# The output projection of a Hymba-style block as seven block products instead of eight

## The chip, the cores and the metric

The kernel runs on one core of a Trainium2 chip. The metric is device time in microseconds (us) of one execution, less is better. PE is the tensor engine, DVE the vector engine, ACT the scalar engine, POOL GpSimd, SP the engine whose queue issues the DMAs.

## The reference, cut to what matters

```python
mod = c_act @ w_ada[l] + b_ada[l]
shift, scale, gate = jnp.split(mod, 3, axis=-1)
h = _rms(x, norm_g[l]) * (1.0 + scale[:, None, :]) + shift[:, None, :]
proj = h @ w_in[l]
...
att = att * jax.nn.silu(a_z)
hg = _hgrn2(g_q, g_f, g_i, lbs[l], hg_norm_g[l]) * jax.nn.silu(g_z)
y = jnp.concatenate([att, hg], axis=-1) @ w_out[l]
x = x + gate[:, None, :] * y
```

1024 tokens, width 2048, all in float32; `w_in` is 2048 x 8192, `w_out` 2048 x 2048. There are 8 attention heads (`att`) and 8 recurrent heads (`hg`), each 128 wide.

## The kernel before

Every large product is made of three matmuls. Each float32 factor is split into a high and a low part: ACT copies it to the rounded type (`whi`), DVE subtracts that from the original (`wlo`). PE then adds high·high, high·low and low·high in PSUM.

The **input projection** goes through slices of `w_in`, four per head pair: `all` twice (q, k, v, i of half the tokens each), `qf` and `zz`. A slice has 16 row blocks of 128 (k tiles), 12 matmuls of 512 columns each. Weight tiles come through a small ring: `W.dma(n + 4)` loads four tiles ahead and `W.split(n + 2)` splits two ahead, with 4 buffers for the raw tile and 3 each for `whi` and `wlo`. The **mixers** of each head (attention, recurrence) are generators, traced in steps between these matmuls. A small planner (`Stream`, `Engine`, `run_ready`) estimates when each engine gets through its instructions and lets a mixer take its next step when its inputs should be there. What is fixed in this way is only the order on each engine; each engine then runs its own list strictly in that order. A further generator, `gate_gen`, forms the residual's gate and stores it to DRAM (`gdr`); it is done early.

The gated outputs of 14 of the 16 heads are put by in DRAM (`odr`) and come back in the last slice, two per k step (`reload_o`), as high and low parts; the last pair stays in SBUF.

The **output projection** multiplies these, 1024 tokens x 2048, with `w_out` in five column blocks (`outs`): two of 256 columns, then three of 512. The 256-wide blocks keep four PSUM banks busy while the last heads' mixers still hold the others; the 512-wide ones take all eight. For each head the ring brings a tile of `w_out`, PE multiplies it with the 8 token tiles, and after 16 heads DVE multiplies with the gate, adds x and SP stores. For the last block the gate is multiplied into `w_out` beforehand. The gate's sums over the partitions (`gate_rows`, the PSUM tile `gb`) are made in the first block:

```python
    outs = [(0, 256), (256, 512)] + [(c0, c0 + 512) for c0 in range(512, D, 512)]
...
            if kk in (8, 10, 12) and c0 == 0:
                gr = gate_rows() if kk == 8 else gr
                next(gr)
```

`big` is a pool of 14 SBUF tiles of 4 KB per partition (`T4`), `hp` one of 32 that holds the split h, later the split outputs.

## Time and profile before

| what | value |
|---|---|
| median of 3 runs | 2079.76 us (2079.02 to 2082.41) |
| profiled execution: first to last instruction (span) | 2077.0 us |
| median above that span | 2.76 us |
| PE busy in the span | 2046.1 us (99%) |
| DVE, ACT, POOL busy | 48%, 30%, 5% |
| DMA | 210.76 MB, mean 101 GB/s |

The span is counted from the first to the last instruction of one profiled execution. Its own device time is not recorded apart from that; what lies around the span is seen only as the 2.76 us by which the median of the other runs is longer. A matmul's record is longer than the distance to the next one, since matmuls are pipelined: its pace is read from start to start.

### The profile page before, as it was taken

Reading aid. Unit: us, or ns where it says so; the run is one execution under the profiler, and the core shown is the slowest. Engines: PE = TensorE matmul, PEld = TensorE weight load, DVE = VectorE, ACT = ScalarE, POOL = GpSimd, SP = SyncE. Lnnn points to the kernel's source line nnn. Section 1 sums busy time; section 2 is a strip of 40 time slices with the busy share of each in tenths; the row PEclk is TensorE's granted clock in tenths of the full one; section 3 lists DMA queues with packets and bytes.
Section 4 is the critical chain, followed back from the end, with each engine's and each line's share of the span. In section 5 each row is a group of like instructions: output and inputs, shape, how many; then the busy total and the mean of one; then the engine's idle time right before and its main releaser. Section 6 shows DMA issues by size and latency. Waiting matters only on the chain.

```text
span 2077.0 us, 30591 instructions
## 1 busy us (share of the span) xinstructions
PE 2046.1 (99%) x11905; PEld 1707.8 (82%) x11905; DVE 989.6 (48%) x1726; ACT 628.8 (30%) x1491; POOL 97.6 (5%) x104
## 2 busy tenths in 40 slices
PE   6999999999999999999999999999999999999999
PEld 4678878888888888888888888888888889988887
DVE  6884654475547443644363436343634384213142
ACT  6454323322431233124312431243134342111110
POOL 2440000000000000000000000000000000000000
PEclk9999999999999999999999999999999999999999
DMA  9982134334433331133113311331133152332231
GB/s 344 338 231 77 44 102 131 90 92 132 130 88 96 111 89 51 42 92 87 48 47 92 89 46 42 98 88 41 42 107 85 47 177 72 107 102 86 92 127 56
DMA packets 282485, 210.76 MB, mean 101 GB/s; under 512 B 17042, under 2 KB 255714, under 8 KB 282340
## 3 DMA queue, kind: packets, MB, share of 16 engines
q1 hardware_dynamic: 282084, 208.75, 33.5%
q8 instruction: 93, 1.52, 0.3%
q14 instruction: 52, 0.43, 0.1%
q0 software_dynamic: 256, 0.06, 0.0%
HBM read 191.96 MB, written 16.79 MB: 101 GB/s over the span
## 4 chain that ended last, share of the span: by engine, by line
PE 96%; DVE 1%; DMA 1%; ACT 0%; issue 0%; POOL 0%; SPq 0%; ACTq 0%; POOLq 0%; DVEq 0%
PE pj L87 63%; PE pjo L87 11%; PE po L87 6%; PE att L87 6%; PE pjn L87 2%; PE pjC L87 2%; PE lv L87 2%; PE hgo L87 1%; PE pjB L87 1%; PE qkT L87 1%; PE hgU L87 1%; DMA x<-in_x_dram 1%; PE xTp L87 1%; DMA wada<-in_w_ada_dram 0%; PE hgoT L87 0%
## 5 line engine op out<-in xcount | busy, mean ns | idle before, releaser
L87 DVE TENSOR_TENSOR wlo<-wraw,whi 128x512 fp32r<-128x512 f32 x440 | 303.2, 690 | 664.0 <-ACT whi L87 662.8
L87 ACT ACTIVATE whi<-wraw 128x512 fp32r<-128x512 f32 x440 | 276.8, 630 | 826.3 <-PE pj L87 514.5
L87 PE MATMUL pj<-hh,whi 128*128 128x512 f32 x1024 | 412.3, 403 | 0.0
L87 PE MATMUL pj<-hl,whi 128*128 128x512 f32 x1024 | 400.3, 391 | 0.0
L87 PE MATMUL pj<-hh,wlo 128*128 128x512 f32 x1024 | 399.7, 390 | 0.0
L87 PE MATMUL pj<-whi,hh 128*128 128x512 f32 x896 | 356.3, 398 | 0.5 <-DVE z L87 0.5
L87 PE MATMUL pj<-whi,hl 128*128 128x512 f32 x896 | 349.7, 390 | 0.0
L87 PE MATMUL pj<-wlo,hh 128*128 128x512 f32 x896 | 349.2, 390 | 0.0
L87 PEld LDWEIGHTS pj<-hl,whi 128*128 128x128 f32 x1024 | 192.2, 188 | 41.8
L87 PEld LDWEIGHTS pj<-hh,whi 128*128 128x128 f32 x1024 | 192.5, 188 | 36.2
L87 PEld LDWEIGHTS pj<-hh,wlo 128*128 128x128 f32 x1024 | 192.8, 188 | 34.2
L87 PEld LDWEIGHTS pj<-whi,hl 128*128 128x128 f32 x896 | 168.2, 188 | 35.7
L87 PEld LDWEIGHTS pj<-whi,hh 128*128 128x128 f32 x896 | 168.5, 188 | 34.4 <-DVE z L87 1.8
L87 PEld LDWEIGHTS pj<-wlo,hh 128*128 128x128 f32 x896 | 168.6, 188 | 31.8
L87 PE MATMUL pjo<-whi,oh 128*128 128x256 f32 (+1 forms) x448 | 147.7, 330 | 0.0
L87 PE MATMUL pjo<-whi,ol 128*128 128x256 f32 (+1 forms) x448 | 147.2, 329 | 0.0
L87 PE MATMUL pjo<-wlo,oh 128*128 128x256 f32 (+1 forms) x448 | 147.2, 328 | 0.0
L87 ACT ACTIVATE P<-att,mstat 128x640 f32<-128x640 f32 (+2 forms) x64 | 42.3, 662 | 167.3 <-DVE mstat L87 167.3
L87 PEld LDWEIGHTS pjo<-wlo,oh 128*128 128x128 f32 x448 | 84.6, 189 | 7.6
L87 PEld LDWEIGHTS pjo<-whi,oh 128*128 128x128 f32 x448 | 84.6, 189 | 7.6
L87 PEld LDWEIGHTS pjo<-whi,ol 128*128 128x128 f32 x448 | 84.6, 189 | 7.5
L87 PE MATMUL po<-whi,oh 128*128 128x512 f32 x192 | 74.7, 389 | 0.0
(223 smaller groups left out, 2283.0 us busy)
## 6 DMA issues: line engine op xcount, KB each, us to landing
wraw<-in_w_in_dram SPq DMA_DIRECT2D x240, 192.0 KB, 2.9
wraw<-in_w_in_dram SPq DMA_DIRECT2D x272, 128.0 KB, 2.6
wada<-in_w_ada_dram SPq DMA_DIRECT2D x64, 512.0 KB, 7.5
wadag<-in_w_ada_dram SPq DMA_DIRECT2D x64, 256.0 KB, 2.9
wraw<-in_w_in_dram SPq DMA_DIRECT2D x240, 64.0 KB, 2.7
wraw<-in_w_out_dram SPq DMA_DIRECT2D x48, 256.0 KB, 2.8
x<-in_x_dram SPq DMA_DIRECT2D x16, 512.0 KB, 10.1
xr<-in_x_dram SPq DMA_DIRECT2D x16, 512.0 KB, 6.5
```

The source lines that it names most:

```text
L87: return f(*a, **kw)
```

## The change

Write A for the heads' outputs and B for `w_out` times the gate. The change cuts A by tokens (first and last 512) and by kind of head (`att`, `hg`), B by kind of head and by column halves of 512 within a group `q` of 1024 columns, so that for each `q` a 2 x 2 by 2 x 2 block product remains. It is formed from seven products instead of eight (Strassen's scheme):

```
M1 = (A11+A22)(B11+B22)   M2 = (A21+A22) B11   M3 = A11 (B12-B22)   M4 = A22 (B21-B11)
M5 = (A11+A12) B22        M6 = (A21-A11)(B11+B12)                  M7 = (A12-A22)(B21+B22)
C11 = M1+M4-M5+M7   C12 = M3+M5   C21 = M2+M4   C22 = M1-M2+M3+M6
```

The right factors are formed by a new generator, `wout_gen`, that runs after the gate has been stored, among the mixers of the middle heads: 16 rounds (2 `q` x 8 `j`), each with two loads of 512 KB of `w_out`, two multiplications with the gate (1024 wide), five additions (512 wide) and seven stores of 256 KB to the DRAM tile `wdr`. The left factors are formed in `out_sums`, five additions per head pair as it comes back (`reload_o`, now four loads of 256 KB). The output projection is then 2 x 7 products of 8 steps; a step loads one right tile (256 KB), splits it, splits one left tile (`ahl`) and does 12 matmuls of 512 columns into four banks, two sets of four in turn. The sums of the M's, x and the stores lie among the steps of M6 and M7 (`finals`), the copies out of PSUM at each product's last step. The last head pair takes its slices in the order `qf`, `all`, `all`, `zz`. Comments were removed as well.

```diff
+OUTPACE = 20.0
...
-                if len(self.specs[self.ns]) == 4:       # times the gate
-                    c0 = self.specs[self.ns][3]
-                    V.tensor_mul(raw, raw, gates[c0 // 1024][:, c0 % 1024:c0 % 1024 + 512].rearrange(
-                        "p (a b) -> p a b", a=2))
...
+    OA = {}
+    def half_tile(j):
+        if j % 2 == 0:
+            OA["half"] = hp.tile([128, 1024], F32, tag="h", name="oah")
+        return OA["half"][:, (j % 2) * 512:(j % 2) * 512 + 512]
+    def out_sums(j, a11, a12, a21, a22):
+        y, z = (hp.tile([128, 1024], F32, tag="h", name=n) for n in ("oay", "oaz"))
+        a7 = half_tile(j)
+        V.tensor_add(y[:, 512:1024], a21, a22)
+        V.tensor_add(y[:, 0:512], a11, a22)
+        V.tensor_add(z[:, 0:512], a11, a12)
+        V.tensor_sub(z[:, 512:1024], a21, a11)
+        V.tensor_sub(a7, a12, a22)
+        OA[j] = {1: y[:, 0:512], 2: y[:, 512:1024], 3: a11, 4: a22, 5: z[:, 0:512], 6: z[:, 512:1024], 7: a7}
     def finish(kt, oT, direct):
         if direct:
-            hi = hp.tile([128, 1024], F32R, tag="h", name=f"oh{kt}")
-            lo = hp.tile([128, 1024], F32R, tag="h", name=f"ol{kt}")
-            A.activation(hi, oT, AF.Copy)
-            V.tensor_sub(lo, oT, hi.bitcast(F32))
-            O[kt] = (hi, lo)
+            O[kt] = oT
+            if len(O) == 2:
+                a, b = O[NH - 1], O[2 * NH - 1]
+                out_sums(NH - 1, a[:, 0:512], b[:, 0:512], a[:, 512:1024], b[:, 512:1024])
         else:
             DMA.dma_start(odr[slot[kt]], oT)
...
+        wait(10.0)
+        yield
+        yield from wout_gen()
+    def wout_gen():
+        for q in range(2):
+            a, hi, lo = T4("gl"), T4("ghi", dt=F32R), T4("glo", dt=F32R)
+            DMA.dma_start(a, gdr[q])
+            A.activation(hi, a, AF.Copy)
+            V.tensor_sub(lo, a, hi.bitcast(F32))
+            yield
+            p = MA("gb")
+            for s in (slice(0, 512), slice(512, 1024)):
+                PE.matmul(p[:, s], onesr.to_broadcast([128, 128]), hi[:, s], start=True, stop=False)
+                PE.matmul(p[:, s], onesr.to_broadcast([128, 128]), lo[:, s], start=False, stop=True)
+            gate = T4("gateb")
+            A.activation(gate, p, AF.Copy)
+            gate = gate.rearrange("p (a b) -> p a b", a=2)
+            yield
+            for j in range(NH):
+                r1, r2 = T4("wor", (128, 2, 512)), T4("wor", (128, 2, 512))
+                for r, e in ((r1, 2 * j), (r2, 2 * j + 1)):
+                    DMA.dma_start(r.rearrange("p a b -> p (a b)"), wout_v[:, order[e], q * 1024:(q + 1) * 1024])
+                wait(OUTPACE)
+                yield
+                V.tensor_mul(r1, r1, gate)
+                yield
+                V.tensor_mul(r2, r2, gate)
+                yield
+                b11, b12, b21, b22 = r1[:, 0, :], r1[:, 1, :], r2[:, 0, :], r2[:, 1, :]
+                for ma, mb, fa, fb in ((1, 3, (V.tensor_add, b11, b22), (V.tensor_sub, b12, b22)),
+                                       (4, 6, (V.tensor_sub, b21, b11), (V.tensor_add, b11, b12))):
+                    o = T4("wos", (128, 2, 512))
+                    fa[0](o[:, 0, :], *fa[1:])
+                    yield
+                    fb[0](o[:, 1, :], *fb[1:])
+                    wait(2.0)
+                    yield
+                    DMA.dma_start(wdr[q, ma - 1, j], o[:, 0, :])
+                    DMA.dma_start(wdr[q, mb - 1, j], o[:, 1, :])
+                    if ma == 1:
+                        DMA.dma_start(wdr[q, 1, j], b11)
+                        DMA.dma_start(wdr[q, 4, j], b22)
+                V.tensor_add(b21, b21, b22)
+                wait(2.0)
+                yield
+                DMA.dma_start(wdr[q, 6, j], b21)
+    def wait(us):
+        Engine.cur.t = max(Engine.cur.t, PE.free) + us
...
-        slices += [("all", h, 0), ("all", h, 1)] if h else []
-        slices += [("qf", h, 0), ("zz", h, 0)]
+        al = [("all", h, 0), ("all", h, 1)] if h else []
+        slices += al + [("qf", h, 0), ("zz", h, 0)] if h < NH - 1 else [("qf", h, 0)] + al + [("zz", h, 0)]
...
-    for c0, c1 in outs:
-        first["o", c0] = len(specs)
-        st_ = 512 // (c1 - c0)
-        for kk in range(0, NK, st_):
-            specs.append((wout_v, tuple(order[kk:kk + st_]), list(range(c0, c1, 128))) + ((c0,) if c1 == D else ()))
...
+    wdr = dr.tile([2, 7, NH, 128, 512], F32, name="wdr")
...
             W.split(n + 2)
     def reload_o(j):
-        kt = order[j]
-        a = T4("orl")
-        DMA.dma_start(a, odr[slot[kt]])
-        hi = hp.tile([128, 1024], F32R, tag="h", name=f"oh{kt}")
-        lo = hp.tile([128, 1024], F32R, tag="h", name=f"ol{kt}")
-        A.activation(hi, a, AF.Copy)
-        V.tensor_sub(lo, a, hi.bitcast(F32))
-        O[kt] = (hi, lo)
+        oa, ob = (odr[slot[order[i]]] for i in (2 * j, 2 * j + 1))
+        x_ = hp.tile([128, 1024], F32, tag="h", name="oax")
+        r = T4("orl")
+        DMA.dma_start(x_[:, 0:512], oa[:, 0:512])
+        DMA.dma_start(x_[:, 512:1024], ob[:, 512:1024])
+        DMA.dma_start(r[:, 0:512], ob[:, 0:512])
+        DMA.dma_start(r[:, 512:1024], oa[:, 512:1024])
+        out_sums(j, x_[:, 0:512], r[:, 0:512], r[:, 512:1024], x_[:, 512:1024])
+    CHAIN = ((2, 0, True), (3, 1, True), (4, 0, False), (5, 1, False), (1, 0, True), (6, 1, True), (7, 0, False))
+    steps = [(q, m, j) for q in range(2) for m, _, _ in CHAIN for j in range(NH)]
+    raws, wsp, asp = {}, {}, {}
+    def right_dma(n):
+        for i in range(len(raws), min(n + 1, len(steps))):
+            q, m, j = steps[i]
+            raws[i] = wp.tile([128, 512], F32, tag="wraw", name="wraw", bufs=4)
+            DMA.dma_start(raws[i], wdr[q, m - 1, j])
+    def right_split(n):
+        right_dma(n)
+        for i in range(len(wsp), min(n + 1, len(steps))):
+            hi = wp.tile([128, 512], F32R, tag="whi", name="whi")
+            lo = wp.tile([128, 512], F32R, tag="wlo", name="wlo")
+            A.activation(hi, raws[i], AF.Copy)
+            V.tensor_sub(lo, raws[i], hi.bitcast(F32))
+            wsp[i] = (hi, lo)
+    def left_split(n):
+        for i in range(len(asp), min(n + 1, len(steps))):
+            _, m, j = steps[i]
+            while j not in OA:
+                PE.free += 0.5
+                run_ready()
+            hl = T4("ahl", (128, 2, 512), F32R)
+            A.activation(hl[:, 0, :], OA[j][m], AF.Copy)
+            V.tensor_sub(hl[:, 1, :], OA[j][m], hl[:, 0, :].bitcast(F32))
+            asp[i] = hl
...
-                    reload_o(2 * kk - 2)
-                    reload_o(2 * kk - 1)
+                    reload_o(kk - 1)
+                if sl == slices[-1] and kk >= 6:
+                    right_dma(2 * kk - 10)
+                    right_split(kk - 6)
+                    left_split(kk - 6)
...
-                    for t in (2 * b, 2 * b + 1):
-                        for i in range(2):
-                            ohi, olo = O[order[kk + i]]
-                            nat_unit(nat[b][:, t % 2, :], ohi, olo, t, w, i, kk + i, t % 2 == 0)
...
+    banks = [[pj.tile([128, 512], F32, tag="pj", name="pjo") for _ in range(4)], None]
+    n = 0
+    for q in range(2):
+        C = {}
+        for m, s_, fresh in CHAIN:
+            if s_ == 1 and banks[1] is None:
                 mx_ctx.__exit__(None, None, None)
                 po_ = ctx.enter_context(tc.tile_pool(name="po", bufs=4, space=PSUM))
+                banks[1] = [po_.tile([128, 512], F32, tag="po", name="po") for _ in range(4)]
+            for j in range(NH):
+                for u in range(4):
+                    if u == 0:
+                        right_dma(n + 4)
+                        right_split(n + 2)
+                    if u == 2:
+                        left_split(n + 2)
+                    right_split(n)
+                    left_split(n)
+                    (whi, wlo), hl = wsp[n], asp[n]
+                    b = banks[s_][u]
+                    ts = slice(u * 128, (u + 1) * 128)
+                    first, last = fresh and j == 0, j == NH - 1
+                    PE.matmul(b, hl[:, 0, ts], whi, start=first, stop=False, skip_group_check=True)
+                    PE.matmul(b, hl[:, 0, ts], wlo, start=False, stop=False, skip_group_check=True)
+                    PE.matmul(b, hl[:, 1, ts], whi, start=False, stop=last, skip_group_check=True)
                     run_ready()
+                    if last:
+                        if m == 2:
+                            if u == 0:
+                                C["v"] = res("cv")
+                            A.activation(C["v"][u], b, AF.Copy, scale=-1.0)
...
+                    elif m in (6, 7) and u in (1, 3):
+                        next(later, None)```

**Start of the output projection, PE.** Rows of the change's instruction order, matmul result<-moving,stationary. Before, the last slice (`pj`) is followed by a step of the last recurrent head's mixer (`lv`) and by 256-wide matmuls, two heads to a tile of weights:

```order
L87 MATMUL pj_13944<-hl15_1616,whi_14205 128x512
L87 MATMUL lv_14321<-hgQ_13914,hgK_13915 32x32 x16
L87 MATMUL pjo_14422<-whi_14253,oh0_14024 128x256
L87 MATMUL pjo_14422<-wlo_14254,oh0_14024 128x256
L87 MATMUL pjo_14422<-whi_14253,ol0_14025 128x256
L87 MATMUL pjo_14422<-whi_14253,oh8_14030 128x256
```

Now the first product, M2, follows at once. The rows are the last of its step 0 and the first three of steps 1 and 2:

```order
L87 MATMUL pjo_14869<-whi_14800,ahl_14804 128x512
L87 MATMUL pjo_14866<-whi_14859,ahl_14863 128x512
L87 MATMUL pjo_14866<-wlo_14860,ahl_14863 128x512
L87 MATMUL pjo_14866<-whi_14859,ahl_14863 128x512
...
L87 MATMUL pjo_14866<-whi_14870,ahl_14890 128x512
L87 MATMUL pjo_14866<-wlo_14871,ahl_14890 128x512
L87 MATMUL pjo_14866<-whi_14870,ahl_14890 128x512
```

No mixer matmul stands in the output projection any more; the last mixer matmul (`att`) stands 57 matmuls ahead of it. In a step the second matmul needs `wlo`, the third the low half of `ahl`, both made by DVE.

**Start of the output projection, DVE.** Before, from the last `z` (the gate path of the last head pair, out of PSUM) on: the low parts of heads 6 and 14 as they come back, then the splits and the last mixers:

```order
L87 SCALAR_TENSOR_TENSOR z_14383<-z_14383,pj_13944 128x512
L87 TENSOR_TENSOR ol6_14413<-orl_14410,oh6_14412 128x1024
L87 TENSOR_TENSOR ol14_14419<-orl_14416,oh14_14418 128x1024
L87 TENSOR_TENSOR wlo_14430<-wraw_14250,whi_14429 128x512
L87 TENSOR_TENSOR hgQ_13914<-hgQ_13914,hgT_13972 128x16x32
L87 TENSOR_TENSOR hgK_13915<-hgK_13915,hgT_13972 128x16x32
L87 TENSOR_TENSOR hgT_13972<-hgT_13972 128x16
L87 SCALAR_TENSOR_TENSOR oT_13277<-oT_13277,z_14366 128x1024
```

Now, from the same `z` on: the five block sums of head pair 6 (`oay`, `oaz`, `oah`), the low parts for steps 1 and 2, and the gating of the last two heads (`oT`):

```order
L87 SCALAR_TENSOR_TENSOR z_14830<-z_14830,pj_14314 128x512
L87 TENSOR_TENSOR oay_14847<-orl_14842,oax_14841 128x512
L87 TENSOR_TENSOR oay_14847<-oax_14841 128x512
L87 TENSOR_TENSOR oaz_14848<-oax_14841,orl_14842 128x512
L87 TENSOR_TENSOR oaz_14848<-orl_14842,oax_14841 128x512
L87 TENSOR_TENSOR oah_14849<-orl_14842,oax_14841 128x512
L87 TENSOR_TENSOR wlo_14860<-wraw_14796,whi_14859 128x512
L87 TENSOR_TENSOR ahl_14863<-oay_14544,ahl_14863 128x512
L87 TENSOR_TENSOR wlo_14871<-wraw_14798,whi_14870 128x512
L87 SCALAR_TENSOR_TENSOR oT_14877<-hgoT_14574,gcol_92,z_14830 128x1024
L87 SCALAR_TENSOR_TENSOR oT_14062<-oT_14062,z_14813 128x1024
```

Right behind them stand the five sums of the last pair (the first row is two instructions), and only then the low half of the left tile of step 2:

```order
L87 TENSOR_TENSOR oay_14880<-oT_14062,oT_14877 128x512 x2
L87 TENSOR_TENSOR oaz_14881<-oT_14062,oT_14877 128x512
L87 TENSOR_TENSOR oaz_14881<-oT_14062 128x512
L87 TENSOR_TENSOR oah_14849<-oT_14877 128x512
L87 TENSOR_TENSOR ahl_14890<-oay_14625,ahl_14890 128x512
```

**The second gate row (`q` = 1), SP.** Before, both loads of the gate's sums (`gl`) stand in the output projection, ahead of the ring's loads and behind two loads of x:

```order
L385 DMA wraw_14638<-in_w_out_dram 128x256 x2
L1050 DMA xr_14722<-in_x_dram 128x4x256
L1050 DMA xr_14724<-in_x_dram 128x4x256
L1007 DMA gl_14726<-gdr_549 128x1024
L1007 DMA gl_14732<-gdr_549 128x1024
L385 DMA wraw_14738<-in_w_out_dram 128x256 x2
```

Now the second one stands among the stores of the last round of `q` = 0, in an `all` slice:

```order
L888 DMA wdr_551<-wos_8704 128x512
L889 DMA wdr_551<-wos_8704 128x512
L389 DMA wraw_8732<-in_w_in_dram 128x2x128 x2
L896 DMA wdr_551<-wor_8420 128x512
L857 DMA gl_8752<-gdr_549 128x1024
L389 DMA wraw_8758<-in_w_in_dram 128x2x128 x2
```

Its matmuls stand one step of the slice after it (12 matmuls of 512 columns). PE before and now:

```order
L87 MATMUL pjo_14425<-whi_14560,ol12_14247 128x256
L87 MATMUL gb_14810<-ghi_14727,onesr_86 128x512
L87 MATMUL gb_14810<-glo_14728,onesr_86 128x512
L87 MATMUL gb_14810<-ghi_14727,onesr_86 128x512
L87 MATMUL gb_14810<-glo_14728,onesr_86 128x512
```

```order
L87 MATMUL pj_8350<-whi_8713,hl14_1529 128x512
L87 MATMUL gb_8777<-ghi_8753,onesr_86 128x512
L87 MATMUL gb_8777<-glo_8754,onesr_86 128x512
L87 MATMUL gb_8777<-ghi_8753,onesr_86 128x512
L87 MATMUL gb_8777<-glo_8754,onesr_86 128x512
```

On DVE the store ahead of `gl` waits for the last addition of the round, and that stands right behind a ring split (`wlo_8714`); ACT's `ghi_8753` and DVE's `glo_8754` (1024 wide) wait for `gl` to land.

## Rows read from the trace of the kernel before

**Rows 1.** The page: span, busy time, chain that ended last by engine

```profile
span 2077.0 us, 30591 instructions
PE 2046.1 (99%) x11905; PEld 1707.8 (82%) x11905; DVE 989.6 (48%) x1726; ACT 628.8 (30%) x1491; POOL 97.6 (5%) x104
PE 96%; DVE 1%; DMA 1%; ACT 0%; issue 0%; POOL 0%; SPq 0%; ACTq 0%; POOLq 0%; DVEq 0%
```

**Rows 2.** Windows: stretch, length, busy PE, PEld, DVE, ACT, POOL, clock, DMA share, GB/s

```profile
170.00:1708.90 1538.90, 1536.31 (x8963) 1282.51 (x8961) 752.44 (x1295) 480.99 (x1195) 36.85 (x22) 1.00 0.29 84
1708.90:1753.37 44.47, 44.47 (x379) 43.91 (x374) 22.39 (x32) 14.21 (x31) 1.64 (x1) 1.00 0.27 84
1753.37:1810.81 57.44, 57.44 (x481) 57.44 (x480) 14.08 (x21) 7.23 (x11) 0.00 (x0) 1.00 0.24 74
1810.81:2072.00 261.19, 261.19 (x1154) 216.03 (x1152) 67.74 (x98) 29.07 (x46) 0.00 (x0) 1.00 0.29 92
2072.00:2077.00 5.00, 0.11 (x1) 0.00 (x0) 0.84 (x2) 0.00 (x0) 0.00 (x0) 0.96 0.66 247
```

**Rows 3.** Waits of PE, 170 to 2077 us, the longest: total, times, longest

```profile
PE hgoT L87 <- DVE hgon L87: 1.4, 1, 1.4
```

**Rows 4.** Timeline of PE (start, length): last of projection, first and last 512-wide of output

```profile
1707.96 0.39 PE L87 MATMUL pj<-hl,whi 128*128 128x512 f32 x1
...
1810.81 0.40 PE L87 MATMUL pjo<-whi,oh 128*128 128x512 f32 x1
...
2071.72 0.39 PE L87 MATMUL po<-whi,ol 128*128 128x512 f32 x1
```

**Rows 5.** Timeline of DVE, end of the last slice

```profile
1709.01 0.69 DVE L87 SCALAR_TENSOR_TENSOR z<-z,pj 128x512 f32<-128x512 f32 x1 [0.67 <-ACT z L87]
...
1712.24 0.68 DVE L87 TENSOR_TENSOR wlo<-wraw,whi 128x512 fp32r<-128x512 f32 x1
1712.84 0.68 DVE L87 TENSOR_TENSOR hgQ<-hgQ,hgT 128x512 f32<-128x512 f32 x1
...
1714.13 1.22 DVE L87 SCALAR_TENSOR_TENSOR oT<-oT,z 128x1024 f32<-128x1024 f32 x1
```

**Rows 6.** Groups by form, DVE and ACT, from 1700 us: busy, mean ns of one

```profile
L87 DVE SCALAR_TENSOR_TENSOR oT<-hgoT,gcol,z 128x1024 f32<-128x1024 f32 x1 | 1.3, 1284 | 3.1 <-PE hgoT L87 3.1
L87 DVE TENSOR_TENSOR glo<-gl,ghi 128x1024 fp32r<-128x1024 f32 x2 | 2.4, 1223 | 0.8 <-ACT ghi L87 0.8
...
L87 ACT ACTIVATE whi<-wraw 128x512 fp32r<-128x512 f32 x63 | 39.8, 631 | 281.1 <-PE po L87 202.0 <-PE pjo L87 51.4 <-DVE wraw L87 14.4
L87 ACT ACTIVATE ghi<-gl 128x1024 fp32r<-128x1024 f32 x2 | 2.0, 1050 | 0.0
```

**Rows 7.** DMA issues: count, KB each, median us to landing

```profile
wraw<-in_w_out_dram SPq DMA_DIRECT2D x48, 256.0 KB, 2.8
...
odr<-oT SPq DMA_DIRECT2D x14, 512.0 KB, 3.0
orl<-odr SPq DMA_DIRECT2D x14, 512.0 KB, 5.2
...
gl<-gdr SPq DMA_DIRECT2D x2, 512.0 KB, 7.3
```

**Rows 8.** Waits of SP's queue for stored outputs: whole span, then 260 to 300 us

```profile
SPq L644 <- DVE oT L87: 124.9, 14, 18.7
...
SPq L644 <- DVE oT L87: 17.3, 1, 17.3
```

**Rows 9.** Waits, 275 to 300 us

```profile
ACT whi L87 <- DMA wraw<-in_w_in_dram: 3.6, 1, 3.6
...
PEld hgoT L87 <- issue: 1.8, 1, 1.8
```

**Rows 10.** Windows at the start of the program

```profile
20.00:30.00 10.00, 6.65 (x40) 5.62 (x39) 9.09 (x25) 8.65 (x19) 1.62 (x3) 0.93 1.07 373
30.00:40.00 10.00, 10.00 (x101) 7.75 (x100) 4.15 (x6) 4.15 (x8) 0.00 (x0) 0.90 1.10 317
```

**Rows 11.** Windows, two of the middle heads

```profile
800.00:1200.00 400.00, 400.00 (x2314) 333.90 (x2313) 179.76 (x315) 120.13 (x299) 8.18 (x5) 1.00 0.24 68
```

151 lines of the change are left out of this document (71 added, 80 removed).

## The prediction

> **What bounds the kernel now.** I read the page first: PE is busy for 99% of the span and makes up 96% of the chain that ended last [rows 1]. Since a matmul's record is longer than the step to the next one, that alone does not show that PE is at its pace, so the waits of PE came next. From 170 us to the end its longest is 1.4 us [rows 3]. PE is the bound from there on, and an edit counts by the PE time that it takes away, as long as PE's inputs keep coming.
>
> The windows by stage then give the price of the output projection. Between 1753.37 and 1810.81 us only 256-wide matmuls run: 480 weight loads in 57.44 us, 0.1197 us a matmul [rows 2]. The 512-wide ones start at 1810.81, the last of them at 2071.72 [rows 4]; there are 2 x 384 in two full blocks and 384 in the third, 1152 in all, so 260.91 / 1151 = 0.2267 us each. Two 256-wide ones cost 0.2394 us, more than one 512-wide. After the last matmul some 5 us pass: a vector addition, a store, its landing [rows 2].
>
> **The change, part by part.**
>
> *Matmuls.* Removed: 2 blocks x 16 heads x 8 token tiles x 3 = 768 of 256 columns, 768 x 0.1197 = 91.9 us, and 1152 x 0.2267 = 261.2 us; together 353.1 us. Added: 2 x 7 products x 8 steps x 12 = 1344 of 512 columns, 1344 x 0.2267 = 304.7 us. The difference is **-48.4 us**. Of it 43.5 come from the eighth product (192 x 0.2267) and 4.9 from the narrow form. The form of the added ones (128 x 512, stationary tile from SBUF) is that of the rows, so the price has no other bound. The eight gate matmuls stay, and so do those of the mixers: they move out of the output projection into the last two slices, where PE pays for them as before.
>
> The Trainium skill, page "TensorE: Matmul & The Clock Gate", section "Back-to-back issue gap", gives N / 2.4 + 2.5 ns from one matmul to the next, 109 ns and 216 ns. By the page the saving would be 768 x 0.1092 + 1152 x 0.2158 - 1344 x 0.2158 = 42.4 us, since there the narrow form costs half the wide one. The rows differ from it at both widths, and the sum keeps to them.
>
> *Start of the output projection.* Here I expect a new wait. The order shows DVE's list from the last `z` on. That `z` can't be earlier: it reads the last PSUM bank of the last slice. In the trace the last matmul of that slice starts at 1707.96 [rows 4]; call its end, 1708.19, T0. The `z` starts at 1709.01, T0 + 0.82 [rows 5]. DVE's 512-wide operations follow each other every 0.60 us (1712.24, 1712.84), one alone lasts 0.69 [rows 5]. So in the new list:
> - five sums of pair 6 start from T0 + 1.42; `wlo` of step 1 starts at 4.42 and is done at 5.11, `ahl` of step 1 at 5.71, `wlo` of step 2 starts at 5.62;
> - the two `oT` (1.28 and 1.22 us [rows 5, 6]) take 6.22 to 8.72, the five sums of pair 7 end their turn at 11.72, and `ahl` of step 2 is done at 12.41.
>
> PE starts step 0 at T0 and needs 2.72 us for it. In step 1 the second matmul is due at 2.95 and waits until 5.11 (2.2 us), the third until 5.71 (0.4). Step 1 ends at 7.98. In step 2 the third matmul is due at 8.43 and waits until 12.41 (4.0). From there on DVE has two splits, 1.2 us, for each 2.72 us of PE and draws ahead again. Sum **+6.5 us**. It would be 7.7 if each of the 13 short operations took its full 0.69, and some 2 more if the loads for pair 5, ahead of the `z`, took 7.3 us to land and not 5.2 [rows 7]. Before, PE had no long wait here [rows 3], because the ring had its splits done two tiles ahead and four large operations stood here, not ten sums.
>
> *Gate rows.* The two `gl` loads now stand in the middle of the program, with ACT's `ghi`, DVE's `glo` and PE's `gb` right behind, and the planner counts no time for a load to land. Behind `ghi` on ACT the next `whi` are queued, behind `glo` the next `wlo`, so PE would wait for these as well, but they are split two steps ahead. For `q` = 1: SP's store ahead of `gl` waits for DVE's addition, which follows a `wlo`, which follows a `whi`, which can start when PE ends a step; call that T1. Then 0.63 [rows 6], 0.60 and 0.69 [rows 5] make T1 + 1.9, the store's issue 2.3. A 512 KB load lands 5.2 us later in the row nearest to it (`orl`), 3.0 for a store of that size and 7.3 for two `gl` behind loads of x [rows 7]. With 5.2, `ghi` (1.05) and `glo` (1.22 [rows 6]) are done at T1 + 9.8. PE reaches the second `gb` matmul three steps and one matmul after T1, at 8.39. Wait **1.4 us**; with 3.0 none, with 7.3 it is 3.5. For `q` = 0 no vector result stands between SP and its `gl` for the last 10 us, SP runs about two steps ahead there, and I take 0, at most the same 3.5.
>
> *Work taken at nothing, and its cover.* In the middle heads DVE is busy for 179.76 of 400 us [rows 11]. A round adds 2 x 1.2 + 5 x 0.60 = 5.4 us, and by the places of the rounds in the order it comes every 36 us or so: 45% becomes 60%. The DMA share there is 0.24 [rows 11]; 2 x 29 MB more (`wdr` written and read) spread over the program leave it far from the 1.1 of the start [rows 10]. In the output projection a step takes DVE two splits and at most two of the final additions: 4 x 0.60 = 2.4 us against PE's 2.72, and ACT 2 x 0.63. The right tile lands in 2.8 us [rows 7] and is asked for two steps, 5.4 us, before its split. If DVE took 0.69 for each, 2.76 us, it would fall behind by 0.04 us a step, nothing against splits that are two steps ahead. The end is as before: one addition, one store of 256 KB.
>
> **Sum.** 2077.0 - 48.4 + 6.5 + 1.4 = 2036.5 us of span. The median of the runs is 2.8 us above the span, which I carry over: **2039 us**, 2.0% faster.
>
> **Rivals.**
>
> *No new wait at the start*: DVE's list is through before PE needs it. Then 2039.3 - 6.5 = 2033. Against it: the last `z` is tied to PE, and 15 operations behind it stand in a fixed order.
>
> *The clock falls in the new wait.* At the start of the program, where PE was busy for 6.65 of 10 us, the granted clock of the next windows was 0.93 and 0.90 [rows 10]: 0.7 + 1.0 = 1.7 us lost. If the wait of 4.0 us does the same, 2041. Against it: the wait of 1.4 us left the clock at 1.00 [rows 2, 3]. By the same page of the Trainium skill, part 1, idleness of PE throttles it to the lower of its two levels until it has been active again; the trace agrees for the start, and no row shows a wait of 4 us in dense work.
>
> *Fuller DVE delays the mixers.* Their places on PE are fixed by estimates; a vector operation of a round that comes late in front of a mixer's makes PE wait up to 0.60 us. The rounds last 16 x 36 us, 2.8 heads, some 22 attention tiles: 22 x 0.60 = 13, **2052 us**. For it: PE's list leaves no second place to go. Against it: the planner counts DVE's time for the rounds.
>
> *The other side: SP's queue.* The seven stores of a round wait on SP for DVE, and the weight loads of the ring stand behind them. At 267 to 285 us SP waited 17.3 us for a head's output [rows 8], the next weights came late, ACT waited 3.6 us for them and PE lost 1.8 [rows 9]. 16 rounds have 48 such groups of stores; at 1.8 us each it would be 86 us, some 2125 us, slower. It decides from 0.8 us a group. Against it: 14 such waits, 124.9 us in all [rows 8], cost PE only this once, and the new stores stand at least 2 us of planned time behind their operation.
>
> *The change doesn't do what it says*: the seventh less is saved on PE, but DVE sets the pace of M6 and M7. If a step there took 0.63 for ACT and 4 x 0.69 in series, 3.39 us, then 0.67 x 28 steps = 19 us more, 2058.
>
> **Chances.** Forecast 0.53; clock falls too 0.12; no wait 0.14; mixers delayed 0.15; SP's queue 0.03; DVE sets the pace 0.03. The predicted time is that of the first. The range, 2031 to 2052, takes in the first four and their bounds and leaves out the last two and the tails. A measurement of this kernel tells about 0.2%, 4 us, from no change. All cases but SP's queue are faster by more: faster 0.96, same 0.01, slower 0.03.
>
> **What the profile after would show.** The matmul counts 1344 with 0.227 us from start to start. Two waits of PE for DVE within 15 us of the first `pjo` matmul, 2 to 3 us and about 4 us, on `wlo` and `ahl`. One wait at `gb` of 0 to 3.5 us near the middle, for `glo`. No wait of PE over 0.7 us elsewhere after 300 us, and the clock at 1.00. I am wrong in the sum if the first `pjo` matmuls run on without a gap, and wrong in kind if PE waits for `whi` behind late `wraw` loads, or if the steps of M6 and M7 are longer than 2.72 us.

## The result, and the profile after

The median fell from 2079.78 to 2050.90 us (2049.85 to 2055.74), a ratio of 0.9867 with a 95% interval of 0.9853 to 0.9881. The prediction was 2039 us. The sign and the larger part of the gain are as forecast; about 12 us of it are missing. The profiled execution has a span of 2048.6 us, where the sum of the prediction came to 2036.5. Single executions of any of these kernels come out some 4 to 4.5 us longer, with a lower clock ahead of 80 us (last section); the profiles of E2, E7, E8 and E12 are among them, so for these the median counts.

The page of the changed kernel, lines as in [rows 1]:

```profile
span 2048.6 us, 30420 instructions
PE 2005.3 (98%) x11329; PEld 1654.9 (81%) x11329; DVE 1182.3 (58%) x2038; ACT 713.8 (35%) x1659; POOL 97.6 (5%) x104
PE 93%; DVE 3%; DMA 2%; ACT 1%; issue 1%; POOL 0%; SPq 0%; ACTq 0%; DVEq 0%; POOLq 0%
```

PE has 576 matmuls less and is still the bound, but its share of the chain fell from 96 to 93%. The chain now leads through DVE and DMA in places, so PE must have waited. All waits of PE from 300 us on that come to more than 0.5 us (engine and tile, what for: total, times, longest); the one of 1.4 us in [rows 3] lies ahead of 300 us, and from there on the kernel before had none:

```profile
PE pjo L87 <- DVE ahl L87: 3.7, 1, 3.7
PE gb L87 <- ACT ghi L87: 2.8, 2, 2.5
PE pjo L87 <- DVE wlo L87: 2.1, 1, 2.1
PE lv L87 <- DVE Amat L87: 1.6, 3, 0.7
PE gb L87 <- DVE glo L87: 1.4, 2, 0.8
PE pj L87 <- ACT v L87: 0.8, 2, 0.4
```

The two waits at `pjo` are those that the prediction worked out. Those at `gb` come at both gate rows. The windows (length, busy PE, PEld, DVE, ACT, POOL, granted clock, DMA share, GB/s) show what followed:

```profile
704.00:708.20 4.20, 1.14 (x4) 0.24 (x3) 1.31 (x2) 1.58 (x2) 0.00 (x0) 0.87 1.00 349
708.20:713.90 5.70, 5.70 (x18) 4.70 (x19) 2.93 (x3) 1.02 (x1) 0.00 (x0) 0.50 0.10 37
1729.70:1742.20 12.50, 6.66 (x27) 4.64 (x26) 11.79 (x19) 4.97 (x9) 0.00 (x0) 0.96 0.14 42
1742.20:1748.20 6.00, 5.99 (x14) 4.73 (x15) 3.02 (x6) 1.15 (x2) 0.00 (x0) 0.50 0.32 87
1748.20:2043.70 295.50, 295.50 (x1304) 244.55 (x1304) 184.44 (x293) 134.63 (x236) 0.00 (x0) 1.00 0.47 145
```

Behind the waits at 704 and at 1730 to 1742 us PE ran at a granted clock of 0.50, the lower of its two levels (1.2 GHz), for some 6 us each time, without any idle time in them: PE busy for 5.70 of 5.70 us. The busy share of PE doesn't show such a loss, the count does: 14 matmuls in 6.0 us, against 26 at the pace of the last row. That row is the output projection from step 3 on (steps are counted from 0): 1304 matmuls of 512 columns in 295.5 us, 0.2266 us each against 0.2267 from [rows 4], with DVE busy for 62% of it. The products M6 and M7 lie in it and stop PE nowhere.

The start of the output projection on DVE (start, length), to be held against the working of the prediction; the last matmul of the last slice starts at 1729.54 us, so T0 is 1729.76:

```profile
1730.59 0.69 DVE L87 SCALAR_TENSOR_TENSOR z<-z,pj 128x512 f32<-128x512 f32 x1 [0.68 <-ACT z L87]
...
1734.20 0.69 DVE L87 TENSOR_TENSOR wlo<-wraw,whi 128x512 fp32r<-128x512 f32 x1
1734.81 0.69 DVE L87 TENSOR_TENSOR ahl<-oay,ahl 128x512 fp32r<-128x512 f32 x1
...
1736.01 1.28 DVE L87 SCALAR_TENSOR_TENSOR oT<-hgoT,gcol,z 128x1024 f32<-128x1024 f32 x1
...
1738.46 1.29 DVE L87 TENSOR_TENSOR oay<-oT 128x512 f32<-128x512 f32 x2
...
1741.47 0.69 DVE L87 TENSOR_TENSOR ahl<-oay,ahl 128x512 fp32r<-128x512 f32 x1
```

The `z` starts at T0 + 0.83 (0.82 was read from [rows 5]), `wlo` of step 1 at T0 + 4.44 (4.42), `ahl` of step 2 ends at T0 + 12.40 (12.41). The order of a strict list and three durations were enough to foretell the sum of these waits to a tenth of a microsecond. On PE:

```profile
1732.26 0.61 PE L87 MATMUL pjo<-whi,ahl 128*128 128x512 f32 x2
1734.95 0.50 PE L87 MATMUL pjo<-wlo,ahl 128*128 128x512 f32 x1 [2.08 <-DVE wlo L87]
1735.55 0.72 PE L87 MATMUL pjo<-whi,ahl 128*128 128x512 f32 x2
...
1738.15 0.39 PE L87 MATMUL pjo<-wlo,ahl 128*128 128x512 f32 x1
1742.21 1.22 PE L87 MATMUL pjo<-whi,ahl 128*128 128x512 f32 x2 [3.68 <-DVE ahl L87]
1743.23 0.63 PE L87 MATMUL pjo<-wlo,ahl 128*128 128x512 f32 x1
1743.66 1.05 PE L87 MATMUL pjo<-whi,ahl 128*128 128x512 f32 x2
1744.51 0.63 PE L87 MATMUL pjo<-wlo,ahl 128*128 128x512 f32 x1
```

The second matmul of the first row starts at 1732.48. From start to start the three gaps, up to 1734.95, 1735.55 and 1742.21, are 2.47, 0.60 and 4.07 us where 0.227 is normal: 2.24 + 0.38 + 3.84 = 6.5 us lost, as predicted. Behind them three matmuls take 1.28 us (1743.23 to 1744.51), 0.427 each.

The gate row of `q` = 0, on SP, ACT and PE (SP's rows: start, length of the issue):

```profile
693.03 0.86 SPq L380 DMA_DIRECT2D wraw<-in_w_in_dram  x1
698.38 0.33 SPq L656 DMA_DIRECT2D odr<-oT  x1
...
701.26 0.38 SPq L857 DMA_DIRECT2D gl<-gdr  x1
```

```profile
705.80 1.06 ACT L87 ACTIVATE ghi<-gl 128x1024 fp32r<-128x1024 f32 x1 [4.76 <-DMA gl<-gdr]
```

```profile
704.06 0.39 PE L87 MATMUL pj<-whi,hl 128*128 128x512 f32 x1
706.91 0.66 PE L87 MATMUL gb<-ghi,onesr 128*128 128x512 f32 x1 [2.46 <-ACT ghi L87]
708.17 0.80 PE L87 MATMUL gb<-glo,onesr 128*128 128x512 f32 x1 [0.60 <-DVE glo L87]
...
713.89 0.43 PE L87 MATMUL pj<-whi,hh 128*128 128x512 f32 x1
```

SP stood from 693.9 to 698.4 us at the store of a head's output, which waits for DVE's `oT`; four weight loads followed, and only then `gl`. PE was through with what stands ahead of `gb` 3.0 us after that issue (704.29), ACT had the data 4.5 us after it. With `gl` issued those 4.4 us earlier, `glo`, done at 708.12, would have been done at 703.7, ahead of its matmul; that is worked out from these rows, since no run takes the store away.

### The profile page after: what moved, and what is told of

Its sections match the earlier page's. It is cut to its first block, busy times and chain, and to the rows that moved or that the text cites. A ratio compares the mean times of both kernels' runs of the same rounds, so it can differ in the third digit from the quotient of the medians.

```text
span 2048.6 us, 30420 instructions
## 1 busy us (share of the span) xinstructions
PE 2005.3 (98%) x11329; PEld 1654.9 (81%) x11329; DVE 1182.3 (58%) x2038; ACT 713.8 (35%) x1659; POOL 97.6 (5%) x104
## 4 chain that ended last, share of the span: by engine, by line
PE 93%; DVE 3%; DMA 2%; ACT 1%; issue 1%; POOL 0%; SPq 0%; ACTq 0%; DVEq 0%; POOLq 0%
PE pj L87 62%; PE pjo L87 8%; PE po L87 6%; PE att L87 6%; PE pjn L87 2%; PE pjC L87 2%; PE lv L87 2%; PE hgo L87 1%; PE pjB L87 1%; DMA x<-in_x_dram 1%; PE qkT L87 1%; PE hgU L87 1%; PE xTp L87 1%; PE hgoT L87 0%; DVE Amat L87 0%
## 5 line engine op out<-in xcount | busy, mean ns | idle before, releaser
L87 DVE TENSOR_TENSOR wlo<-wraw,whi 128x512 fp32r<-128x512 f32 x488 | 336.2, 690 | 483.0 <-ACT whi L87 478.1
L87 ACT ACTIVATE whi<-wraw 128x512 fp32r<-128x512 f32 x488 | 307.3, 630 | 733.1 <-PE pj L87 500.9
L87 PE MATMUL pj<-hh,whi 128*128 128x512 f32 x1024 | 411.8, 402 | 0.4 <-ACT v L87 0.4
L87 PE MATMUL pj<-hl,whi 128*128 128x512 f32 x1024 | 400.0, 391 | 0.0
L87 PE MATMUL pj<-hh,wlo 128*128 128x512 f32 x1024 | 399.6, 390 | 0.0
L87 PE MATMUL pj<-whi,hh 128*128 128x512 f32 x896 | 357.9, 399 | 0.9 <-DVE z L87 0.5
L87 PE MATMUL pj<-whi,hl 128*128 128x512 f32 x896 | 350.3, 391 | 0.0
L87 PE MATMUL pj<-wlo,hh 128*128 128x512 f32 x896 | 349.7, 390 | 0.0
L87 PEld LDWEIGHTS pj<-hl,whi 128*128 128x128 f32 x1024 | 192.2, 188 | 41.6
L87 PEld LDWEIGHTS pj<-hh,whi 128*128 128x128 f32 x1024 | 192.5, 188 | 36.8 <-ACT v L87 0.8
L87 PEld LDWEIGHTS pj<-hh,wlo 128*128 128x128 f32 x1024 | 192.8, 188 | 34.3
L87 PEld LDWEIGHTS pj<-whi,hl 128*128 128x128 f32 x896 | 168.5, 188 | 36.2
L87 PEld LDWEIGHTS pj<-whi,hh 128*128 128x128 f32 x896 | 168.8, 188 | 35.3 <-DVE z L87 1.8
L87 PEld LDWEIGHTS pj<-wlo,hh 128*128 128x128 f32 x896 | 168.9, 188 | 31.6
L87 PE MATMUL pjo<-whi,ahl 128*128 128x512 f32 x512 | 161.2, 394 | 3.8 <-DVE ahl L87 3.7
L87 PE MATMUL po<-whi,ahl 128*128 128x512 f32 x384 | 119.2, 389 | 0.0
L87 PEld LDWEIGHTS pjo<-whi,ahl 128*128 128x128 f32 x512 | 97.3, 190 | 25.0 <-DVE ahl L87 4.5
L87 PE MATMUL pjo<-wlo,ahl 128*128 128x512 f32 x256 | 100.7, 393 | 2.1 <-DVE wlo L87 2.1
L87 ACT ACTIVATE P<-att,mstat 128x640 f32<-128x640 f32 (+2 forms) x64 | 42.4, 662 | 165.6 <-DVE mstat L87 165.6
L87 PEld LDWEIGHTS po<-whi,ahl 128*128 128x128 f32 x384 | 72.1, 188 | 15.0
L87 PE MATMUL po<-wlo,ahl 128*128 128x512 f32 x192 | 74.7, 389 | 0.0
L87 PEld LDWEIGHTS att<-PT,v 128*128 128x128 f32 x480 | 63.1, 191 | 5.6
## 6 DMA issues: line engine op xcount, KB each, us to landing
wada<-in_w_ada_dram SPq DMA_DIRECT2D x64, 512.0 KB, 8.1
wraw<-wdr SPq DMA_DIRECT2D x112, 256.0 KB, 2.7
wadag<-in_w_ada_dram SPq DMA_DIRECT2D x64, 256.0 KB, 2.8
wor<-in_w_out_dram SPq DMA_DIRECT2D x32, 512.0 KB, 5.5
wdr<-wos SPq DMA_DIRECT2D x64, 256.0 KB, 2.1
```

The source lines that it names most:

```text
L87: return f(*a, **kw)
```

## The experiments

All ratios are to the kernel before, timed on the same chip in turn. "Span" is that of the profiled execution.

### E1: the gate rows later

```diff
-            a, hi, lo = T4("gl"), T4("ghi", dt=F32R), T4("glo", dt=F32R)
+            a = T4("gl")
             DMA.dma_start(a, gdr[q])
+            wait(8.0)
+            yield
+            hi, lo = T4("ghi", dt=F32R), T4("glo", dt=F32R)
             A.activation(hi, a, AF.Copy)
```

> Edit: behind the load of a gate row (gl) the planner now waits 8 us before it places ghi, glo and the gb matmuls, for both q; nothing else. Theory (PE waited at gb for the landing of gl, and the clock fell behind that wait at q = 0): in the changed kernel the stretch from 704.06 to 713.89 us holds 3.4 us of matmuls and transposes at full clock and so 6.4 us of loss, the one at 998.6 us 0.5 + 1.0 + 0.1 = 1.6 us. Both go: 8.0 us less, a span of about 2040.6, no granted clock below 1.00 near the middle. Rival A (the clock there falls for another reason than the wait): only the waits go, 2.6 + 1.0 + 1.6 = 5.2 us, span 2043.4, and a stretch at 0.427 us a matmul stays. Rival B (the wait follows gb, since it is SP that is behind its plan): no gain, the same wait some 8 us later.

2040.82 us, ratio 0.9820 (0.9806 to 0.9833), span 2038.9. Both waits at `gb` and the slow stretch behind the first are gone (the clock is 1.00 from 704 to 760 and from 990 to 1040 us): of the theory's 8.0 us and Rival A's 5.2 the gain, 9.7 from span to span, leaves only the first: the slow clock there came from the wait. There is a second finding. At the start of the output projection nothing was changed, and PE waits there for the same 2.24 + 0.38 us in step 1. But now the clock falls right behind these, not only behind the wait of step 2, and that wait shrinks from 3.84 to 2.23 us, since PE comes to it later. The first 48 matmuls there lose 8.3 us against the pace of 0.2267, and 9.5 in the changed kernel: 1.2 of the 1.7 us by which the gain is larger than the theory's. Another 0.8 us are gained ahead of the first `pj` matmul (159.89 us for 160.68), which the edit doesn't touch (windows of E1: length, busy PE, clock, DMA share, GB/s):

```profile
1723.80:1727.20 3.40, 1.22 (x5) 0.99 0.00 0
1727.20:1737.40 10.20, 8.14 (x22) 0.67 0.35 95
```

### E2: the sums of the last two pairs later

```diff
+SUMSAT = {1: 6, 3: 7}
...
-        out_sums(j, x_[:, 0:512], r[:, 0:512], r[:, 512:1024], x_[:, 512:1024])
+        held[j] = x_[:, 0:512], r[:, 0:512], r[:, 512:1024], x_[:, 512:1024]
+        if j < NH - 2:
+            out_sums(j, *held.pop(j))
...
                     if u == 2:
                         left_split(n + 2)
+                    if u == 3 and n in SUMSAT:
+                        out_sums(SUMSAT[n], *held.pop(SUMSAT[n]))
```

`finish` puts the arguments of the last pair into `held` in the same way.

> Edit: the five sums of pair 6 are issued in step 1 of the output projection instead of ahead of it, those of pair 7 in step 3 instead of with the last oT. DVE's operations are the same in number. Theory (DVE's list of 15 operations behind the last z makes PE wait 2.24 + 0.38 + 3.84 us, and the clock falls behind these waits): by the working of the prediction z ends at T0 + 1.4, wlo of step 1 at 2.1 (due 2.95), wlo of step 2 at 3.3, two oT at 5.8, ahl of step 2 at 6.4 (due 8.4 or later): no wait of PE, and 6.46 us go; 5.8 us at half the clock go too, another 2.9 us. 9.4 us less, span about 2039.2. Rival A (the clock falls at the start of the output projection for another reason): 6.5 us less, span 2042.1, a stretch at 0.427 us a matmul stays. Rival B (DVE is simply short of time there, and the sums only move the wait to steps 3 to 5): at most 3 us less.

2041.18 us, ratio 0.9827 (0.9813 to 0.9840). The profiled execution has 2045.5 us of span, the three others 2039.1 to 2039.6, against 2039.2 expected. One wait of 0.3 us is left at `pjo`, and the clock is 1.00 through the stretch (windows: length, busy PE, clock, DMA share, GB/s):

```profile
1005.00:1009.50 4.50, 3.98 (x11) 0.65 0.30 96
...
1728.00:1760.00 32.00, 31.75 (x141) 1.00 0.33 99
```

Rivals A and B are out: without the waits the clock stays, and DVE has the time, only its order was bad. In this execution the second gate row made PE wait longer (1.7 + 1.0 us from start to start; 0.5 + 1.0 in the changed kernel) and the clock fell there too (0.65 from 1005 to 1009.5 us).

### E3: both

> Both edits, that of the gate rows and that of the sums. Theory: the two stalls are far apart and add up: 8.0 + 9.4 = 17.4 us less than the changed kernel, span about 2031.2. Rival A (the clock falls for reasons other than waits): 11.7 us less, 2036.9. If the span is more than 3 us above what the two single edits give together, they are not independent.

2033.60 us (2033.21 to 2034.17), ratio 0.9783 (0.9770 to 0.9797), span 2031.8. The gains add up to within 2.2 us: the two single spans (2039.3 for E2) would give 2029.6, within the 3 us that were set for this. E1's 1.2 us at the start of the output projection can't be gained a second time. This version beats both kernels. Of PE's waits after 300 us the largest group and the one at the start of the output projection are these:

```profile
PE lv L87 <- DVE Amat L87: 0.9, 2, 0.7
...
PE pjo L87 <- DVE ahl L87: 0.3, 1, 0.3
```

### E4: one product twice

```diff
-    CHAIN = ((2, 0, True), (3, 1, True), ...
+    CHAIN = ((2, 0, True), (2, 0, True), (3, 1, True), ...
...
-        for m, s_, fresh in CHAIN:
+        for ci, (m, s_, fresh) in enumerate(CHAIN):
...
-                    if last:
+                    if last and ci:
```

> Edit: M2 is made twice in each half of the columns, the first result is dropped: eight products of block sums instead of seven, with the same sums, loads and final additions, and with 8 steps more of splits and loads each. Theory (a product costs its matmuls, 96 x 0.2267 = 21.8 us for each half): 43.5 us more, span 2092.1. Rival A (DVE sets part of the pace in the products): more than 45 us. Rival B (the start of the output projection has slack to give, the wait for the sums of pair 7 lies in the first eight steps anyway): less than 42 us. With the theory, the -43.5 us of the prediction's first term hold and the missing 12 us lie elsewhere.

2092.48 us, ratio 1.0063 (1.0049 to 1.0077): an eighth product takes away more than the gain. From the first `pjo` matmul to the end it takes 361.2 us for 318.8, 42.4 more, and its first 48 matmuls lose 8.3 us where the changed kernel loses 9.5: without that difference 43.6, so the 43.5 of the prediction holds. In the window from 1747 to 2086 us there are 1497 matmuls in 339.00 us, 0.2265 each.

### E5: only the sums of the last pair later

E2 with `SUMSAT = {3: 7}`; the sums of pair 6 stay ahead of step 1.

> Edit on the changed kernel: only the sums of pair 7 are put off to step 3; those of pair 6 stay ahead of step 1. Theory (each wait follows from the place of its operation in DVE's list): the waits on wlo and ahl of step 1 stay at 2.2 and 0.4 us, the one on ahl of step 2 falls from 3.8 to about 1.0, since ahl of step 2 now ends at T0 + 9.4 and is due at 8.4. If the clock falls behind a wait of 2.2 + 0.4 us already, as it did in the run with the gate rows put later, the stretch at 0.427 us stays and the gain is 2.8 us (span 2045.8); if it needs the longer wait, 5.7 us (2042.9).

2044.35 us, ratio 0.9843 (0.9822 to 0.9863), span 2042.6: the second of the two numbers. The wait in step 1 stays as it was (2.1 us in the view), the one in step 2 falls to 0.66 us from start to start, and the clock keeps 1.00 (8 us windows of E5):

```profile
1732.00:1740.00 8.00, 5.33 (x22) 1.00 0.23 66
1740.00:1748.00 8.00, 8.00 (x37) 1.00 0.36 98
```

So the same 2.24 + 0.37 us were followed by a lower clock in E1 and not here.

### E6: pauses between the operations of a round

E3 with `wait(2.0)` behind each `tensor_mul` and behind the first addition of each pair. It was made for two waits of 0.87 us at `lv`, behind a round's operations on DVE, here in the changed kernel:

```profile
879.09 1.22 DVE L87 TENSOR_TENSOR wor<-wor,gateb 128x1024 f32<-128x1024 f32 x1
880.35 1.29 DVE L87 TENSOR_TENSOR wos<-wor 128x512 f32<-128x512 f32 x2
...
883.01 1.79 DVE L87 COPY_PREDICATED Amat<-masks,lv 32x256 f32<-32x256 uint8 x4
```

```profile
884.94 0.47 PE L87 MATMUL lv<-hgQ,hgK 128*64 128x64 f32 x9 [0.71 <-DVE Amat L87]
```

> Edit on the version with both mendings: 2 us of planned time are put between the vector operations of a round of the right factors, which stood back to back. Theory (two waits of PE on Amat, 0.87 us each at 883 and 1092 us of the changed kernel, stand behind a tensor_mul and two additions of a round on DVE): both vanish, a gain of up to 1.7 us against the version with both mendings, span about 2030.1, too little for the clockless comparison of medians but seen in the list of gaps. Rival (they are the head's own): they stay. With 8 us more for each round, the rounds may meet other places of the mixers: then small waits of the same size come up elsewhere and the sum of the gaps stays near 4 us.

2035.03 us, ratio 0.9787 (0.9773 to 0.9802), span 2033.4: no gain. The first of the two waits falls from 0.83 us, its size in E3, to 0.37. The second had gone in E3 already, where the rounds start 8 us later, so this run says nothing of it. Others came: 1.0 at the second gate row, 1.0 at a `pj` at 1105 us, and the sum of the gaps is 5.2 us for 4.0 in E3. The rival's second half fits, that the rounds meet the mixers elsewhere.

### E7: the last pair's slices in their old order

E1 with `slices += al + [("qf", h, 0), ("zz", h, 0)]` for every head.

> Edit on the version with only the gate rows mended: the slices of the last pair in their old order (all, all, q | f, zz), so the recurrence of the last head starts about 175 us later. Theory (the new order is what lets pair 7 be ready): in the kernel before, the last oT of that head came 37 us behind the last matmul of the last slice; five sums (3.0) and a split (0.6) follow it, and PE's list is fixed: PE waits in step 5 or 6 for that chain, 10 to 20 us with the clock falling behind it, so a span of 2049 to 2062. The small waits at 1578 to 1609 us (0.3 + 0.4 + 0.6) vanish. Rival (the mixer's steps find room between the products as they did before): within 3 us of the version it is made from, 2036 to 2042.

2047.81 us, ratio 0.9854 (0.9839 to 0.9869), 7.0 us more than E1. The last recurrence now runs inside the output projection, and PE waits at three steps of its chain (waits of PE from 1690 us on):

```profile
PE hgoT L87 <- DVE hgon L87: 6.5, 1, 6.5
PE hgo L87 <- DVE hgS L87: 2.7, 1, 2.7
PE hgU L87 <- ACT hgKN L87: 1.0, 1, 1.0
...
```

That is 10.2 us of new waits, at the low end of what was expected. The loss is smaller, and the other executions' spans, 2044.4 to 2046.6, lie below the range I gave: the waits of the first steps shrink, since `ahl` of step 2 no longer stands behind the sums of pair 7. The new order of the slices is thus part of what lets the products start.

### E8: the stores of the right factors at once

```diff
                     fb[0](o[:, 1, :], *fb[1:])
-                    wait(2.0)
                     yield
...
                 V.tensor_add(b21, b21, b22)
-                wait(2.0)
                 yield
```

> Edit on the changed kernel: the 2 us of planned time between the last vector operation of a group and its stores are left out, so the stores of wdr stand on SP as soon as their operation is issued. Theory (SP has slack, the weight loads are asked for two steps ahead): SP's waits for DVE grow, PE's do not: the time stays within 3 us, span 2046 to 2052. Rival (SP's queue, the case on the other side of the prediction): each of 48 groups delays the weight loads behind it, ACT waits for wraw and PE for whi, from 0.5 us a group or 24 us on.

2081.96 us, ratio 1.0011 (0.9997 to 1.0025): some 30 us more than the changed kernel, the whole gain is gone. My theory fell here. The case on the other side of the prediction, SP's queue, is real in this run, and these two lines keep it away. The worst place, SP and then ACT of this run:

```profile
913.71 0.85 SPq L380 DMA_DIRECT2D wraw<-in_w_in_dram  x1
918.83 0.33 SPq L887 DMA_DIRECT2D wdr<-wos  x1
...
919.82 1.50 SPq L890 DMA_DIRECT2D wdr<-wor  x1
...
923.51 1.32 SPq L872 DMA_DIRECT2D wor<-in_w_out_dram  x2
924.92 0.42 SPq L389 DMA_DIRECT2D wraw<-in_w_in_dram  x1
```

```profile
932.17 0.63 ACT L87 ACTIVATE whi<-wraw 128x512 fp32r<-128x512 f32 x1 [7.96 <-DMA wraw<-in_w_in_dram]
```

SP stands 4 us at a store, then issues seven stores and two loads for 6 us, and the next weight load comes 11 us behind the one before. The split stands 8 us, the `hgon` of a head is queued behind it on DVE, and PE waits 5.8 us for that and then runs at the lower clock (0.52 from 934 to 941 us).

### E9 to E12: what of E8 it was

E8 changes three things: stores earlier on SP, rounds denser, operations and stores in bunches. E9 keeps the 2 us but behind the stores; E10 sets `OUTPACE = 14.0`; E11 puts the seven operations back to back on DVE, with the stores in groups 2 us apart; E12 keeps the operations apart and issues the seven stores in one bunch.

> Edit on the changed kernel: the 2 us of planned time between an operation and the stores behind it stay, but now follow the stores. The rounds keep their pace and PE its list, word for word; only the places of the stores on SP move ahead. It takes apart the two things that the run without the 2 us changed. Theory (SP stands at the stores until DVE has done their operation, and the weight loads behind come late): ACT waits longer for wraw, PE behind it, and most of the 31 us come back: span above 2062. Rival (the denser rounds did it, 31 us apart in place of 36): the time stays within 3 us of the changed kernel, 2046 to 2052.

> Edit on the changed kernel: OUTPACE 14 in place of 20, so the rounds come some 30 us apart, as in the run without the 2 us, but with the 2 us in their place. Theory (SP's early stores cost the time there): small changes only, where other places of the mixers are met, span 2045 to 2055. Rival (the denser rounds cost it): above 2065.

> Edit on the changed kernel: the seven vector operations of a round stand back to back on DVE, its stores come behind them in three groups, 2 us of planned time apart and 2 us behind the last operation. The run without the 2 us lost 31 us; neither earlier stores alone nor denser rounds alone did. Two things are left: seven operations in one bunch on DVE, or seven stores in one bunch on SP. Theory (the bunch on SP: a weight load stands behind seven stores and two loads, 6 us of issue): this run loses little, span 2045 to 2055. Rival (the bunch on DVE: 5.4 us of operations in front of a wlo or of a mixer's operation): span above 2065.

> Edit on the changed kernel: the vector operations of a round keep their 2 us apart, its seven stores come in one bunch on SP, 2 us of planned time behind the last operation, with the two loads of the next round right behind. Theory (the bunch on SP): weight loads come late and ACT waits for wraw, span above 2060. Rival (the bunch on DVE): span 2045 to 2055. If neither this run nor the one with the operations in a bunch loses, it takes SP's standing at a store for DVE and the bunch together.

| run | median us | ratio, interval | ACT waits for `wraw`, 700 to 1300 us |
|---|---|---|---|
| changed kernel | 2050.90 | 0.9867, 0.9853 to 0.9881 | 11.4 us |
| E8 | 2081.96 | 1.0011, 0.9997 to 1.0025 | 21.2 us |
| E9 stores earlier | 2053.43 | 0.9881, 0.9865 to 0.9898 | 22.3 us |
| E10 denser rounds | 2052.42 | 0.9878, 0.9863 to 0.9892 | 13.9 us |
| E11 operations bunched | 2053.09 | 0.9876, 0.9862 to 0.9891 | 23.4 us |
| E12 stores bunched | 2061.06 | 0.9909, 0.9893 to 0.9926 | 22.4 us |

The intervals of E9, E10 and E11 overlap that of the changed kernel. Only the bunch of stores costs by itself, some 9 us by the ratios, and of the four only E12 has PE waiting for `whi`. ACT's waits for `wraw` don't tell the runs apart: E9 and E11 have as many as E12. Waits of PE in E12:

```profile
PE pj L87 <- ACT whi L87: 3.4, 2, 1.8
```

By the numbers E9's rival and the theories of E10 and E11 came out. But E9's rival blamed the denser rounds and E10's theory the early stores, and each of these runs clears what the other blames: neither costs by itself. E12 came out between its theory and its rival (spans 2064.7, 2059.2, 2055.9 and 2059.4 us, where above 2060 and up to 2055 were expected). The bunch on SP is the largest part of E8 that a single run shows; some 20 of its 30 us are not assigned to one of the three alone. PE doesn't wait for `whi` in E8, so that its loss comes by the way of E12's is not shown either, and that the three need each other is argued from the single runs, not shown.

## Why the prediction was off by 12 us

**The matmuls, -48.4 us: right.** The pace of 0.2267 us holds over 1304 matmuls, and E4 measured the eighth product at 43.6 us for 43.5. With the two stalls mended (E3) 2031.8 us of span are left. The prediction's 2077.0 - 48.4 is 2028.6, and the list of E3's gaps from start to start holds some 4.0 us more than before. That makes 2032.6 and leaves the matmul term within 1 us. The Trainium skill, page "TensorE: Matmul & The Clock Gate", section "Back-to-back issue gap", would give 192 x 0.2158 = 41.4 us for E4 (an estimate by its formula, which the page gives for the isolated matmul, as the prediction does not say); the measured pace decides.

**The start of the output projection, +6.5: right**, 2.24 + 0.38 + 3.84 us, and E2 and E5 show that it is DVE's order that makes it.

**The gate row of `q` = 1, +1.4: right**, 0.51 + 1.03 + 0.11 = 1.7 us in gaps from start to start, though 0.5 of it at the first `gb` matmul, where none was expected (E1 takes it away with the other).

**The gate row of `q` = 0, "I take 0": the first step that failed.** It cost 6.5 us: the stretch from 704.06 to 713.89 us holds eleven matmuls of 512 columns, 2.5 us at 0.2267, and eight transposes, which take 0.8 us in the next head; it lasts 9.8. Of the loss 3.65 us are waits and 2.9 the lower clock. The reason I gave was that no vector result stands between SP and its `gl` and that SP runs two steps ahead. The trace of after shows the store of a head's output, `odr`, four loads ahead of `gl`, and SP waiting 4.4 us there for DVE's `oT`. The upper bound that I noted, 3.5 us, is close to the waits; I should have priced it, since all that I had against it was that stretch of the queue, and I had read it wrongly.

**The clock, 0: the second step that failed.** I had it as a rival of 12%, in one place and for 1.7 us. It fell in two places and cost 2.9 us each: from 1742.21 to 1748.26 us 14 matmuls took 6.05 us instead of 3.17. My argument against it was that the wait of 1.4 us in [rows 3] left the clock alone; that row says nothing of longer waits, or of several close together, and both places have these. E1, E2 and E3 show that without the waits it does not fall. My price for the wait of 4 us, 1.7 us, came from the start of the program (where, besides, the 0.93 in [rows 10] belongs to the ten microseconds with the idle time and not to the next ones) and was too low. By the Trainium skill, page "TensorE: Matmul & The Clock Gate", part 1, idleness of PE throttles it to its lower level until it has been active again. The traces agree with that in kind, 0.50 behind the waits and 1.00 some 6 us later.

**The mixers, "no wait over 0.7 us elsewhere": too small by 3.6 us.** Six small gaps of 0.27 to 0.87 us came up, two of them (0.87 each) behind a round's operations on DVE, three in the last pair's slices (0.27, 0.38 and 0.59 us; E7 with the old order has none of these), one of 0.59 behind the second gate row. The rival's mechanism is seen at the first two, and its 22 places of 0.60 us were wrong; the three come with the new order of the slices, which the prediction took at nothing.

Together 6.5 + 2.9 + 3.6 + 0.3 = 13.3 us more than in the sum, against 12.1 found; the list is 1.2 us too long, and of that only some 0.4 us are placed, at the end (4.9 us from the start of the last matmul, 5.3 before).

That the measured time still lies within 2031 to 2052 us is luck: the upper end stood there for the mixers' 13 us, and these came to 3.6, while most of the miss came from two terms at nothing.

**The rivals.** *No new wait* is out. *DVE sets the pace* is out: no gap in 295 us. *SP's queue* did not come. The 2 us of planned time that I named do keep it away, since without them (E8) some 30 us are lost, where I had 86; but not because the stores stand behind them, for E9 has the stores first and loses nothing clear of noise. The 1.8 us a group in that price were read from a weight load's row in [rows 9]; PE itself waited 1.4 us there [rows 3], which makes 67 us.

## What to carry to other kernels

When a load is moved into the middle of dense work, read from the order what stands ahead of it on the DMA queue, back to the last transfer that waits for an engine; a planner that counts no time for landing puts the consumer on PE too early, and 8 us of planned delay took that loss away here. A stall of PE in dense work may cost more than its length: here 3.7 us of waits cost 6.5 and 6.5 cost 9.3, and neither the busy share nor the waits show the rest, only the granted clock and the distance of the starts. Work that is needed late (here the sums of the last pairs) belongs behind work that is needed now on a strict list, and stores that wait for results belong in small groups between loads: all seven of a round in one bunch cost some 9 us here.
